# A decoder layer on one core: the embedding projection moved between the output products and the gate products, and weight blocks asked for one unit ahead

## The chip, the cores and the metric

The kernel runs on one core of one Trainium2 chip. The core has five engines that run side by side and wait for each other through semaphores: TensorE (matmuls, called PE in the profile, its weight loads PEld), VectorE (DVE), ScalarE (ACT), GpSimd (POOL) and SyncE (SP), whose queue here starts nearly all transfers between HBM and the on-chip memory. Matmuls write to eight banks of accumulators (PSUM); all else lives in the on-chip memory (SBUF). Each engine takes its instructions in the order in which the built program lists them.

The metric is the time of one execution in device microseconds, as the median of several runs. Less is better.

## What is computed

The reference is one layer of a decoder, 1024 tokens of width 1024 in float32. Cut to the parts that matter here:

```python
# h is the residual after attention: h = x + merged @ w_out
n2 = rms_norm(h, g_ffn)                                   # per token, over 1024
h = h + (silu(n2 @ w_ffn_gate) * (n2 @ w_ffn_up)) @ w_ffn_down   # D_FF = 2816
e = rms_norm(p @ w_ple_proj, g_ple)                       # p: 1024 x 256, w_ple_proj: 256 x 1024
h = h + sigmoid(h @ w_ple_gate) * e
out = rms_norm(h, g_final)
```

The embedding projection `p @ w_ple_proj` depends on inputs alone. Its result, and the per-token scale of its norm, are needed only at the very end.

## The kernel before, in words

All activations lie transposed: features over the 128 partitions, tokens along the free axis in two halves of 512 (`hf`, `hcol(hf)`). To keep float32 accuracy each operand of a matmul is split into a high part, rounded by ScalarE, and the low rest, subtracted by VectorE (`split`, lines 131 and 132), and each product is three matmuls: high by high, high by low, low by high (`passes`, lines 137 to 139). So a matmul waits for ScalarE's half of its operand, and every third one for VectorE's.

The order of the program's work: attention; the merge and the output products `po` (`w_out`, the second half of them in `out_group`); the norm's scales and the factors for the next products; gate and up products; down products; the embedding's gate and the final norm.

**Gate and up products.** They use a Strassen-Winograd scheme: for every block of 256 output features, called a unit, seven products of half size (128 x 512, four terms in the sum, so 12 matmuls of 128x512 each) take the place of eight. The right factors `Bn[1]` to `Bn[7]` (`b` in the profile) are built once from the normed `h`, in the order 1, 2, 5, 6, 7, 3, 4 that the products take them. The left factors are built for each unit from its weight block `raw` (1 MB, three buffers, tag `raw`) by sums on GpSimd (lines 918, 919, 935, 937) and then split into one of three buffers `wl`. There are 22 units, gate and up by turns, numbered `u` from 0. The first three (two gate units and an up unit, `us`) run together, product by product, since they wait for the right factors at the same time; the other 19 come from `rest()`, one after the other, with the last two products of a unit behind the first two of the next. An up unit multiplies its result with the gate's (on GpSimd, line 983), subtracts further sums on VectorE (line 976), and SP stores seven blocks per pair to `d_g` (line 973).

**Down sums.** The down products use the same scheme, so four sums of `w_ffn_down`'s blocks are formed for each of 11 values of `kk` (`down_sums`): four loads of 256 KB (line 1094), four VectorE operations (line 1097), four stores to `d_w` (line 1098). Before, a round belongs to each of the first 11 units of `rest()`, with its loads at the same place as its sums, into tiles of the ring `t` (16 buffers).

**The embedding.** `embed(hf)` loads its half of `p` and the whole of `w_ple_proj` in eight pieces, splits them, and makes eight tiles `pp` of six matmuls. ScalarE copies each (line 1072) and squares it (line 1073); the copy is stored to `d_e`, and four column sums with `ones` (line 1064, tile `pm`, on the chip eight matmuls of 128x1) add up the squares for the norm. Before, the two halves stand in the loop of `rest()`, after its units 7 and 13.

**What sets the order.** The code lists the work; a scheduler then orders the instructions of each engine at build time by a model of their times and by priority, which is the place in the code, raised in `tc.high_priority`. So an instruction can move far ahead of its place when its operands and its buffer are free. The three places shown with the change come from the built programs.

**Memory.** Eight slots of 16 KB per partition (tag `big`) go round: gate tiles, the merged activations `mT`, `wo`, then `spare` and the seven `Bn`. `spare` holds eight tiles of 512: the first four are the first snapshots of the first three units (`early_tile`), the last four `t2`, a Strassen factor; later it takes the first eight left blocks of the down products (line 1116).

## Time and profile before

| what | value |
|---|---|
| median of 3 runs | 1810.48 us (1808.75 to 1811.49) |
| the profiled execution | 1808.15 us, its span on the core 1806.4 us |
| TensorE busy | 1703.0 us, 94% of the span |
| VectorE, ScalarE, GpSimd busy | 1182.2, 906.9, 373.7 us |
| moved to and from HBM | 152.98 MB read, 67.90 MB written |
| gate and up blocks, from request to landing | 5.4 and 6.6 us in the median, 1 MB each |

How to read it: times count from the span's start. In a row of the timeline stand start, duration, engine, line, operation, written tile and read tiles, and in brackets the idle time of the engine before it and who ended it. In a table of stretches stand for each engine the busy time and the number of instructions, then the granted TensorE clock as a share of full speed and the DMA engines' share. Neighbouring matmuls overlap, so the time from start to start, not the duration, tells their rate. The last output product starts at 959.06, the first down product at 1474.25; what lies between is the part that the change touches.

### The profile page before, as it was taken

To read this page: it belongs to the slowest core of one execution; us is meant where nothing else is said; L and a number is where in the kernel's file an instruction comes from. 1 tells how busy PE (TensorE), PEld (TensorE's weight loads), DVE (VectorE), ACT (ScalarE), POOL (GpSimd) and SP (SyncE) were. 2 spreads that over 40 slices of the span, in tenths; PEclk is the share of its full clock that TensorE was granted. 3 is DMA by queue.
4 is the path that set the end of the run, shared out by engine and by line. 5 is a ranking of instruction groups with operands and counts; after the bars stand their busy time and mean duration, and the time that the engine had idled before them with its cause. 6 is when DMAs were issued, how large, how long until landed. Compare 5 with 4: busy or idle time off the path is not lost.

```text
span 1806.4 us, 23396 instructions
## 1 busy us (share of the span) xinstructions
PE 1703.0 (94%) x8148; PEld 1411.8 (78%) x8148; DVE 1182.2 (65%) x2077; ACT 906.9 (50%) x1762; POOL 373.7 (21%) x401
## 2 busy tenths in 40 slices
PE   6999999999999999996997899989899999999996
PEld 5888878888787888875886677768778878887795
DVE  6676787777876667776469766654643455556655
ACT  5275677666765767765224433333334334445421
POOL 2021210000212433332104133324323410000000
PEclk9999999999998999997998999999999999999998
DMA  5211222212314111218841265564523328664522
GB/s 169 65 58 42 55 57 59 70 53 88 111 42 153 54 60 36 65 59 315 301 159 35 83 204 193 191 211 162 192 81 132 110 93 320 192 194 164 169 70 77
DMA packets 172345, 223.21 MB, mean 124 GB/s; under 512 B 23426, under 2 KB 104322, under 8 KB 172226
## 3 DMA queue, kind: packets, MB, share of 16 engines
q1 hardware_dynamic: 166194, 201.78, 34.6%
q0 software_dynamic: 6032, 19.93, 3.0%
q8 instruction: 64, 1.05, 0.3%
q14 instruction: 55, 0.45, 0.1%
HBM read 152.98 MB, written 67.90 MB: 122 GB/s over the span
## 4 chain that ended last, share of the span: by engine, by line
PE 70%; DVE 10%; DMA 7%; issue 6%; POOL 3%; ACT 2%; SPq 1%; DVEq 0%; POOLq 0%; ACTq 0%
PE pt L137 5%; PE pt L138 5%; PE pt L139 5%; PE pd L137 4%; PE pd L138 4%; PE pd L139 4%; DMA t<-w_ffn_down 2%; PE pP L139 2%; PE pP L137 2%; PE pP L138 2%; PE tp L651 2%; DVE t L976 2%; PE po L137 1%; PE pg L139 1%; PE pg L137 1%
## 5 line engine op out<-in xcount | busy, mean ns | idle before, releaser
L137 PE MATMUL pt<-nTh,w_h 128*128 128x512 f32 (+1 forms) x480 | 191.1, 399 | 3.4 <-ACT go L355 2.3
L138 PE MATMUL pt<-nTl,w_h 128*128 128x512 f32 (+1 forms) x480 | 188.8, 393 | 0.0
L139 PE MATMUL pt<-nTh,w_l 128*128 128x512 f32 (+1 forms) x480 | 187.9, 393 | 0.0
L132 DVE TENSOR_TENSOR wl<-raw,wl 128x512 fp32r<-128x512 f32 x132 | 110.5, 837 | 117.1 <-ACT wl L131 116.7
L139 PE MATMUL pP<-b,wl 128*128 128x512 f32 x352 | 140.3, 401 | 17.2 <-DVE wl L132 17.2
L131 ACT CAST wl<-raw 128x512 fp32r<-128x512 f32 x132 | 82.1, 622 | 131.5 <-PE pP L139 63.3
L137 PE MATMUL pP<-b,wl 128*128 128x512 f32 x352 | 141.5, 402 | 4.5 <-ACT wl L131 2.6
L138 PE MATMUL pP<-b,wl 128*128 128x512 f32 x352 | 140.0, 398 | 0.0
L137 PEld LDWEIGHTS pt<-nTh,w_h 128*128 128x128 f32 (+1 forms) x480 | 90.0, 188 | 25.6 <-ACT go L355 5.6
L139 PEld LDWEIGHTS pt<-nTh,w_l 128*128 128x128 f32 (+1 forms) x480 | 89.9, 187 | 19.3
L138 PEld LDWEIGHTS pt<-nTl,w_h 128*128 128x128 f32 (+1 forms) x480 | 89.9, 187 | 18.1
L138 PE MATMUL pd<-drs,dls 128*128 128x512 f32 x296 | 102.2, 389 | 1.0 <-DVE drs L132 1.0
L139 PE MATMUL pd<-drs,dls 128*128 128x512 f32 x296 | 102.0, 389 | 0.0
L132 DVE TENSOR_TENSOR drs<-drr,drs 128x512 fp32r<-128x512 f32 x74 | 50.9, 691 | 77.3 <-ACT drs L131 77.3
L137 PE MATMUL pd<-drs,dls 128*128 128x512 f32 x296 | 99.5, 392 | 0.4 <-ACT dls L131 0.4
L131 ACT CAST drs<-drr 128x512 fp32r<-128x512 f32 x74 | 46.0, 624 | 101.5 <-PE pd L139 99.0
L139 PEld LDWEIGHTS pP<-b,wl 128*128 128x128 f32 x352 | 68.0, 193 | 35.3 <-DVE wl L132 21.0
L637 POOL TENSOR_SCALAR pw<-pw,st 128x128 f32<-128x128 f32 (+5 forms) x48 | 75.1, 1570 | 71.3 <-DVE st L633 20.1
L137 PEld LDWEIGHTS pP<-b,wl 128*128 128x128 f32 x352 | 67.8, 193 | 20.9 <-ACT wl L131 4.1
L138 PEld LDWEIGHTS pP<-b,wl 128*128 128x128 f32 x352 | 68.1, 193 | 14.1
L445 DVE TENSOR_TENSOR sz<-sz,T 128x512 f32<-128x512 f32 (+2 forms) x96 | 52.3, 550 | 35.2 <-PE T L443 34.4
L356 POOL DMA_DIRECT2D d_gate<-go x32 | 17.8, 556 | 260.9 <-ACT go L355 221.8
(371 smaller groups left out, 4831.2 us busy)
## 6 DMA issues: line engine op xcount, KB each, us to landing
d_g<-t SPq DMA_DIRECT2D x74, 256.0 KB, 2.1
drr<-d_g SPq DMA_DIRECT2D x74, 256.0 KB, 2.9
w_raw<-w_in SPq DMA_DIRECT2D x33, 512.0 KB, 4.2
raw<-w_ffn_gate SPq DMA_DIRECT2D x11, 1024.0 KB, 5.4
raw<-w_ffn_up SPq DMA_DIRECT2D x11, 1024.0 KB, 6.6
t<-w_ffn_down SPq DMA_DIRECT2D x44, 256.0 KB, 4.0
d_w<-t SPq DMA_DIRECT2D x44, 256.0 KB, 2.2
drr<-d_w SPq DMA_DIRECT2D x44, 256.0 KB, 2.7
```

The costliest lines, as they stand in the source:

```text
L131: nc.scalar.copy(out=h, in_=src)
L132: eng.tensor_tensor(out=l, in0=src, in1=r32(h), op=ALU.subtract)
L137: nc.tensor.matmul(ps, lhsT=ah, rhs=bh, start=first and i == 0, stop=False, **kw)
L138: nc.tensor.matmul(ps, lhsT=ah, rhs=bl, start=False, stop=False, **kw)
L139: nc.tensor.matmul(ps, lhsT=al, rhs=bh, start=False, stop=last and i == n - 1, **kw)
L356: nc.gpsimd.dma_start(out=dst, in_=go[0:rows, :])
L445: nc.vector.tensor_tensor(out=sz[:, c0:], in0=sz[:, c0:], in1=T[:, c0:], op=ALU.subtract)
L637: nc.gpsimd.tensor_scalar(out=pw[:, 0:nk], in0=pw[:, 0:nk], scalar1=st[:, 6:7], scalar2=None, op0=ALU.mult)
L651: nc.tensor.transpose(tp[:, i * P:(i + 1) * P], rows[i][:, kb * P:(kb + 1) * P], ident)
L976: nc.vector.tensor_tensor(out=dst, in0=a, in1=b, op=ALU.subtract)
```

## The change

It does four things.

1. The embedding's inputs are loaded and split right after the residual's loads, once: `w_ple_proj` into `wpj`, a slot of the ring `big` that stands ahead of `spare`, and both halves of `p` into two of the three `raw` buffers.
2. Both halves of the embedding are written between the output products and the gate products. Its tiles `e`, which hold copy and square side by side, share the three `wl` buffers; its `pp` tiles take four banks (`A`) and `pm` one of `B`.
3. Gate and up blocks: at the start only unit 0's is asked for; unit 1's after the first half of the embedding, which frees a `raw` buffer, unit 2's after the second. In `rest()` each block is asked for one unit ahead.
4. Down blocks go into `spare`, into its first or last four tiles by turns, asked for one unit ahead of their sums, from the third unit of `rest()` on; the down products' own loads into `spare` move behind the last round.

```diff
@@ -833,7 +833,7 @@
     def gate_up_raw(u):
         return raw_unit((w_ffn_gate, w_ffn_up)[u % 2], u // 2)
 
-    raws = {u: gate_up_raw(u) for u in range(3)}
+    raws = {0: gate_up_raw(0)}
     hs = {}
     Bn = {}
 
@@ -848,6 +848,46 @@
         for hf in range(2):
             hs[f, hf] = t_tile()
             nc.sync.dma_start(out=hs[f, hf], in_=d_h[f * P:(f + 1) * P, hcol(hf)])
+
+    wpj = slot("wpj", [P, 2, 2, D])
+    pw = []
+
+    def embed_in():
+        for k in range(2):
+            raw = wk.tile([P, 2, HALF], F32, name="praw", tag="wl", bufs=3)
+            nc.sync.dma_start(out=raw, in_=w_ple_proj[k * P:(k + 1) * P, :].rearrange("p (c n) -> p c n", n=HALF))
+            for c in range(2):
+                split(wpj[:, 0, k, hcol(c)], wpj[:, 1, k, hcol(c)], raw[:, c, :])
+        for hf in range(2):
+            pw.append(wk.tile([P, 2, 2, HALF], F32R, name="pw", tag="raw", bufs=3))
+            raw = wk.tile([P, 2, HALF], F32, name="praw", tag="wl", bufs=3)
+            nc.sync.dma_start(out=raw, in_=pT[:, hcol(hf)].rearrange("(k p) n -> p k n", p=P))
+            split(pw[hf][:, 0], pw[hf][:, 1], raw)
+
+    def embed(hf):
+        pt = ps.tile([P, HALF], F32, name="pm", **B)
+        es = []
+
+        def column_sums(f):
+            for i in range(4):
+                nc.tensor.matmul(pt[:, i:i + 1], lhsT=es[f][:, 1, i * P:(i + 1) * P], rhs=ones, start=f + i == 0,
+                                 stop=f == 7, skip_group_check=True)
+
+        for f in range(NK):
+            fs = slice(f * P, (f + 1) * P)
+            pp = ps.tile([P, HALF], F32, name="pp", **A)
+            passes(pp, [((wpj[:, 0, k, fs], wpj[:, 1, k, fs]), (pw[hf][:, 0, k, :], pw[hf][:, 1, k, :])) for k in range(2)])
+            e = wk.tile([P, 2, HALF], F32, name="e", tag="wl", bufs=3)
+            nc.scalar.copy(out=e[:, 0, :], in_=pp)
+            nc.scalar.activation(out=e[:, 1, :], in_=pp, func=AF.Square, scale=1.0 / 32.0)
+            nc.sync.dma_start(out=d_e[fs, hcol(hf)], in_=e[:, 0, :])
+            es.append(e)
+            if f:
+                column_sums(f - 1)
+        column_sums(7)
+        rstd_finish(pt, r_ple[:, 4 * hf:4 * hf + 4])
+
+    embed_in()
     spare = slot("spare", [P, 8, HALF], F32)
     t2 = [spare[:, 4 + kk, :] for kk in range(4)]
 
@@ -1002,6 +1042,10 @@
         t = next(early, None)
         return t_tile() if t is None else t
 
+    embed(0)
+    raws[1] = gate_up_raw(1)
+    embed(1)
+    raws[2] = gate_up_raw(2)
     sl = {}
     us = [gate_unit(raws[0], FIRST, early_tile, sl), up_unit(0, raws[1], FIRST, early_tile, sl)]
     sl = {}
@@ -1034,64 +1078,32 @@
 
     def rest():
         global_sl = sl
+        nxt = gate_up_raw(3)
         for u in range(3, NFF):
-            raw = gate_up_raw(u)
+            raw = nxt
+            if u + 1 < NFF:
+                nxt = gate_up_raw(u + 1)
             if u % 2:
                 yield up_unit(u // 2, raw, ORDER, t_tile, global_sl)
             else:
                 global_sl = {}
                 yield gate_unit(raw, ORDER, t_tile, global_sl)
 
-    def embed(hf):
-
-        pw = wk.tile([P, 2, 2, HALF], F32R, name="pw", tag="raw", bufs=3)
-        for k in range(2):
-            praw = t_tile()
-            nc.sync.dma_start(out=praw, in_=pT[k * P:(k + 1) * P, hcol(hf)])
-            split(pw[:, 0, k, :], pw[:, 1, k, :], praw)
-        raws = [t_tile()[:, 0:256].rearrange("p (k n) -> p k n", n=P) for _ in range(NK)]
-        for f, raw in enumerate(raws):
-            nc.sync.dma_start(out=raw, in_=w_ple_proj[:, f * P:(f + 1) * P].rearrange("(k p) n -> p k n", p=P))
-        ws = []
-        for raw in raws:
-            ws.append(wk.tile([P, 2, 2, P], F32R, name="wpj", tag="t", bufs=16))
-            split(ws[-1][:, 0], ws[-1][:, 1], raw)
-        pt = ps.tile([P, HALF], F32, name="pm", **O)
-        sqs = []
-
-        def column_sums(f):
-            for i in range(4):
-                nc.tensor.matmul(pt[:, i:i + 1], lhsT=sqs[f][:, i * P:(i + 1) * P], rhs=ones, start=f + i == 0,
-                                 stop=f == 7, skip_group_check=True)
-
-        for f in range(NK):
-            fs = slice(f * P, (f + 1) * P)
-            pp = ps.tile([P, HALF], F32, name="pp", **B)
-            passes(pp, [((ws[f][:, 0, k, :], ws[f][:, 1, k, :]), (pw[:, 0, k, :], pw[:, 1, k, :])) for k in range(2)])
-            e, sq = t_tile(), t_tile()
-            nc.scalar.copy(out=e, in_=pp)
-            nc.scalar.activation(out=sq, in_=pp, func=AF.Square, scale=1.0 / 32.0)
-            nc.sync.dma_start(out=d_e[fs, hcol(hf)], in_=e)
-            sqs.append(sq)
-            if f > 1:
-                column_sums(f - 2)
-        column_sums(6)
-        column_sums(7)
-        rstd_finish(pt, r_ple[:, 4 * hf:4 * hf + 4])
-
     KK = NFF // 2
     wd = w_ffn_down.rearrange("(k two p) n -> two p k n", two=2, p=P)
 
     def down_block(f, kh, kk):
         return wd[kh, :, kk, hcol(f)]
 
-    def down_sums(kk):
-
-        a = {}
-        for f in range(2):
-            for kh in range(2):
-                a[f, kh] = t_tile()
-                nc.sync.dma_start(out=a[f, kh], in_=down_block(f, kh, kk))
+    def down_in(kk):
+
+        a = {(f, kh): spare[:, 4 * (kk % 2) + 2 * f + kh, :] for f in range(2) for kh in range(2)}
+        for (f, kh), t in a.items():
+            nc.sync.dma_start(out=t, in_=down_block(f, kh, kk))
+        return a
+
+    def down_sums(kk, a):
+
         for i, dst, x, y, op in ((5, (1, 1), (1, 0), (1, 1), ALU.add), (7, (1, 0), (0, 0), (1, 0), ALU.subtract),
                                  (6, (0, 0), (1, 1), (0, 0), ALU.subtract), (3, (0, 1), (0, 1), (0, 0), ALU.subtract)):
             nc.vector.tensor_tensor(out=a[dst], in0=a[x], in1=a[y], op=op)
@@ -1100,8 +1112,11 @@
     LEFT = {5: 0, 6: 1, 7: 2, 3: 3}
     DIRECT = {1: (0, 0), 2: (0, 1), 4: (1, 1)}
     before = None
+    blocks = {}
     for n, u in enumerate(rest()):
 
+        if 2 <= n < KK + 2:
+            blocks[n - 2] = down_in(n - 2)
         for _ in range(2):
             next(u)
         for _ in before or ():
@@ -1109,13 +1124,11 @@
         for _ in range(3):
             next(u)
         before = u
-        if n < KK:
-            down_sums(n)
-        if n == 2:
+        if 3 <= n < KK + 3:
+            down_sums(n - 3, blocks.pop(n - 3))
+        if n == KK + 4:
             for kk in range(0, 8, 2):
                 nc.sync.dma_start(out=spare[:, kk:kk + 2, :], in_=wd[0, :, kk:kk + 2, hcol(0)])
-        if n in (7, 13):
-            embed(n // 8)
 
 
     TAGS = {"rr": ("c", 4), "rs": ("wl", 3), "ls": ("wl", 3)}
```

Where it moves instructions, as the built programs list them (`x` is the number of like rows in sequence):

TensorE at the end of the output products (`po`). Before, the first gate product (`pP`, reading the factor `b` and a left factor `wl`) follows at once:

```order
L138 MATMUL po<-mT_8838,wo 128x256
L139 MATMUL po<-mT_8838,wo 128x256
L137 MATMUL pP<-b_9222,wl 128x512
L138 MATMUL pP<-b_9222,wl 128x512
L139 MATMUL pP<-b_9222,wl 128x512
```

With the change the broadcast of a scale and then the embedding follow:

```order
L139 MATMUL po<-mT_8838,wo 128x256
L738 MATMUL bc<-acc,ones_pp 128x256
L137 MATMUL pp<-pw,wpj 128x512
L138 MATMUL pp<-pw,wpj 128x512
L139 MATMUL pp<-pw,wpj 128x512
```

All 96 matmuls of the embedding and its column sums stand here now, ahead of the first gate product.

SP around the first blocks asked for after that. With the change, from the embedding's stores on:

```order
L883 DMA d_e<-e 128x512 x4
L830 DMA raw<-w_ffn_up 128x8x256
L883 DMA d_e<-e 128x512 x9
L830 DMA raw<-w_ffn_gate 128x8x256
L883 DMA d_e<-e 128x512
L1102 DMA spare<-w_ffn_down 128x512 x4
L1110 DMA d_w<-spare 128x512 x2
L1102 DMA spare<-w_ffn_down 128x512
L1110 DMA d_w<-spare 128x512
L1102 DMA spare<-w_ffn_down 128x512
```

The blocks of units 1 and 2 stand behind the embedding's stores. The scheduler has drawn the down blocks of the rounds with odd `kk`, whose half of `spare` is free first, ahead of all stores of the units; loads and stores alternate in the queue, since a load follows the store of the tile that it overwrites. Unit 3's block stands behind 18 of these loads in all.

VectorE in the first three units, with the change (`L968` adds to a snapshot, `L1109` is a down sum, `wl` the low half of a left factor):

```order
L132 TENSOR_TENSOR b_9244<-spare,b_9244 128x256 x8
L132 TENSOR_TENSOR b_9245<-t,b_9245 128x512 x4
L132 TENSOR_TENSOR b_9246<-t,b_9246 128x512
L1109 TENSOR_TENSOR spare<-spare 128x512
L132 TENSOR_TENSOR b_9246<-t,b_9246 128x512 x2
L968 TENSOR_TENSOR spare<-pR,spare 128x512
L132 TENSOR_TENSOR b_9246<-t,b_9246 128x512
L1109 TENSOR_TENSOR spare<-spare 128x512
L132 TENSOR_TENSOR wl<-raw,wl 128x512
L132 TENSOR_TENSOR b_9247<-t,b_9247 128x512 x4
L1109 TENSOR_TENSOR spare<-spare 128x512
L132 TENSOR_TENSOR wl<-raw,wl 128x512
```

Down sums now stand among the factors and left halves of the first three units; before, the first of them stood among those of the fourth.

## The prediction

> **What bounds the kernel now.** I read the page first, then stretches of the one place that the change touches, then the chain and the waits inside them.
>
> ```profile
> PE 1703.0 (94%) x8148; PEld 1411.8 (78%) x8148; DVE 1182.2 (65%) x2077; ACT 906.9 (50%) x1762; POOL 373.7 (21%) x401
> PE 70%; DVE 10%; DMA 7%; issue 6%; POOL 3%; ACT 2%; SPq 1%; DVEq 0%; POOLq 0%; ACTq 0%
> ```
>
> TensorE sets the pace on the whole, but 94% busy does not say where it loses time. The next view does: from the last output product (959) to the end of the gate and up products (1474), cut where the kind of work changes, and a saturated stretch from the down products for scale. A second answer counts the column-sum matmuls (tile pm) in the two embedding stretches.
>
> ```profile
> core 0: us, PE busy (x) PEld busy (x) DVE busy (x) ACT busy (x) POOL busy (x), PEclk, DMA share, GB/s
> 959.00:1013.00 54.00, 38.80 (x135) 26.71 (x135) 52.81 (x98) 25.42 (x52) 21.15 (x15) 0.88 0.11 35
> 1013.00:1201.00 188.00, 179.76 (x780) 147.05 (x779) 116.09 (x145) 63.13 (x109) 67.36 (x46) 0.99 0.54 179
> 1201.00:1231.00 30.00, 22.79 (x120) 18.96 (x119) 12.05 (x19) 15.38 (x32) 4.51 (x3) 0.89 0.62 208
> 1231.00:1352.80 121.80, 115.95 (x500) 94.78 (x500) 66.34 (x84) 39.73 (x69) 45.10 (x31) 0.97 0.44 148
> 1352.80:1381.00 28.20, 25.70 (x143) 21.39 (x142) 9.81 (x15) 15.70 (x33) 7.08 (x5) 1.00 0.64 209
> 1381.00:1474.00 93.00, 92.03 (x405) 75.54 (x403) 42.43 (x61) 33.03 (x57) 34.49 (x24) 1.00 0.22 76
> 1500.00:1600.00 100.00, 100.00 (x443) 82.81 (x442) 55.78 (x89) 42.01 (x74) 0.00 (x0) 1.00 0.70 230
> ...
> 1201.00:1231.00 30.00, 6.08 (x53) 6.77 (x54) 0.00 (x0) 0.89 0.62 208
> 1231.00:1352.80 121.80, 1.43 (x13) 1.45 (x12) 0.15 (x1) 0.97 0.44 148
> 1352.80:1381.00 28.20, 7.57 (x64) 8.37 (x64) 0.00 (x0) 1.00 0.64 209
> ```
>
> The saturated row gives the price of a full matmul: 100/443 = 0.226 us. A column sum costs 6.08/53 = 0.115 us. What a stretch is longer than its matmuls at these prices is what it loses: 959 to 1013 holds some 120 full matmuls and 15 small ones, 28.6 us of work, and loses 25.4. 1013 to 1201: 780 × 0.226 = 176, loses 12. 1201 to 1231: 67 full and 53 small, 21, loses 9. 1231 to 1352.8: 487 and 13, 111.3, loses 10.5. 1352.8 to 1381: 79 and 64, 25, loses 3. 1381 to 1474: 405, 91.4, loses 1.6. Together **61.5 us lost of 515**; the rest of the program is not touched.
>
> Who takes them? In the first stretch VectorE is busy 52.8 of 54 us, and the chain of waits there (955 to 1020) is mostly its operations, the splitting of the Strassen factors (b) first:
>
> ```profile
> by line: DVE b L132 17.9%; DVE wl L132 11.6%; DVE t L845 9.8%; PE pP L139 8.7%; PE pP L137 6.4%; PE pP L138 6.3%; DVE acc L869 6.1%; issue 5.7%; DVE spare L891 4.3%; DVE t L884 4.1%; DVE acc L735 3.8%; DVE t L1020 3.7%; DVE spare L928 2.8%;
> ```
>
> In the loop a late weight block does it. Here is the longest stall, on four engines (start, duration, what ended the idle time):
>
> ```profile
> 1105.14 0.38 SPq L830 DMA_DIRECT2D raw<-w_ffn_gate  x1
> 1110.72 1.75 POOL L918 TENSOR_TENSOR s<-raw 128x512 f32<-128x512 f32 x1 [1.15 <-DMA d_w<-t]
> 1112.43 1.29 POOL L983 TENSOR_TENSOR t<-t 128x512 f32<-128x512 f32 x1
> 1113.76 2.48 DVE L976 TENSOR_TENSOR t<-t 128x512 f32<-128x512 f32 x2 [2.44 <-POOL t L983]
> 1118.09 0.50 PE L139 MATMUL pP<-b,wl 128*128 128x512 f32 x1 [3.64 <-DVE wl L132]
> ```
>
> The gate block is asked for at 1105.1. GpSimd's sum over it waits until 1110.7; the product of gate and up queues behind that sum on GpSimd, VectorE's subtraction waits for the product, and the low half of the next weights stands behind the subtraction. In the waits of 850 to 1500 the same shows in total, and the embedding's own wait beside it:
>
> ```profile
> PE pP L139 <- DVE wl L132: 17.2, 9, 3.6
> PE pp L137 <- ACT wpj L131: 8.1, 3, 6.5
> POOL s L918 <- DMA raw<-w_ffn_gate: 32.8, 7, 14.2
> SPq L973 <- POOL t L983: 134.7, 13, 19.8
> DVE t L1097 <- DMA t<-w_ffn_down: 17.7, 11, 2.9
> ```
>
> **The embedding leaves the loop.** Its inputs are now asked for and split during the output products, so its first matmul no longer waits for them:
>
> ```profile
> 1208.00 0.80 PE L137 MATMUL pp<-pw,wpj 128*128 128x512 f32 x1 [6.54 <-ACT wpj L131]
> 1209.02 0.63 PE L137 MATMUL pp<-pw,wpj 128*128 128x512 f32 x1
> 1209.44 0.63 PE L138 MATMUL pp<-pw,wpj 128*128 128x512 f32 x1
> 1211.65 0.39 PE L137 MATMUL pp<-pw,wpj 128*128 128x512 f32 x1
> 1211.88 0.39 PE L138 MATMUL pp<-pw,wpj 128*128 128x512 f32 x1
> L1072 ACT COPY t<-pp x16: 576/586/598, 1212.0 to 1375.3; 128x512 f32<-128x512 f32 x16
> L1073 ACT ACTIVATE t<-pp x16: 594/603/625, 1212.5 to 1375.8; 128x512 f32<-128x512 f32 x16
> ```
>
> After the 6.5 us gap matmuls start 0.42 us apart for 3.6 us, then 0.23: a gap costs its own length and the half clock behind it, which my 9 us hold. The work itself stays: 96 × 0.226 + 128 × 0.115 = 36.4 us of TensorE. ScalarE's two operations per tile are 0.59 + 0.60 = 1.2 us against 6 × 0.226 + 8 × 0.115 = 2.3 us of TensorE, so they hide, and with two `e` slots free (the third is held by `acc`) the store's 2.2 us fits into two tiles. Kept lost: 1.5 us; bounds 0 and 6, the last if the copies queue behind ScalarE's casts of the factors as long as that gap. The embedding pieces lost 9 + 3 = 12: **−10.5** (−12 to −6). The splits of its inputs (eight of 0.6 us on each of ScalarE and VectorE) fall under the output products, where both were a third to a half busy:
>
> ```profile
> 850.00:950.00 100.00, 100.00 (x504) 85.17 (x503) 52.21 (x86) 30.10 (x43) 10.65 (x5) 1.00 0.68 242
> ```
>
> Without that cover they would cost 5 us.
>
> **It lands where VectorE is the bound.** TensorE now has 36.4 + 28.6 = 65 us of work over the stretch in which VectorE has 52.8 and a few down sums. So VectorE should cease to be the bound, if the order lets it work ahead. By the order it does most of its factors of b5 during the embedding, then blocks on the third weight block, which is asked for only when the second half's `pw` is read out, just before the last column sums. Prices:
>
> ```profile
> raw<-w_ffn_gate SPq DMA_DIRECT2D x11, 1024.0 KB, 5.4
> t<-w_ffn_down SPq DMA_DIRECT2D x44, 256.0 KB, 4.0
> d_w<-t SPq DMA_DIRECT2D x44, 256.0 KB, 2.2
> 1004.15 5.50 DVE L132 TENSOR_TENSOR b<-t,b 128x512 fp32r<-128x512 f32 x9
> 1208.68 2.10 DVE L132 TENSOR_TENSOR wpj<-t,wpj 128x256 fp32r<-128x256 f32 x6 [0.27 <-ACT wpj L131]
> ```
>
> A split is 5.50/9 = 0.61 us on VectorE, a half one 0.35. Let E be the end of the embedding's column sums. The block is asked for some 2.5 us before E and lands at E + 2.9; its low half is ready at E + 4.2, and TensorE wants it after two units' first products, 24 × 0.226 = E + 5.4: no stall. Then VectorE has, in its order, one weight split, eight half splits of b6 (2.8), four of b7 (2.4), four of b3 (2.4), two down sums and an addition before the second unit's second low half: E + 14.7. TensorE wants that at 4 products × 2.7 + eight matmuls = E + 12.7: stall 2.0. Behind it b4 (2.4) and a down sum precede the third unit's: about 1 more. Ahead of these, ScalarE's high halves cost up to 1. I take **5 us** lost in place of 25.4, **−20.4**. Bounds: 2 (only the first stall) and 18 (VectorE finds only its work on b5, some 30% of the stretch, ready during the embedding, and the other 70% of the old loss returns after it).
>
> **Down sums are the added wait.** Eleven rounds of four sums are no longer held to the units from the fourth on; five of them stand in VectorE's queue among the first three units' weight splits, which wait behind them, and TensorE behind those. A round's cycle is known from here:
>
> ```profile
> 1197.84 1.86 SPq L1094 DMA_DIRECT2D t<-w_ffn_down  x4
> 1204.22 1.42 DVE L1097 TENSOR_TENSOR t<-t 128x512 f32<-128x512 f32 x2 [2.04 <-DMA t<-w_ffn_down]
> ```
>
> From the first request to the first sum 6.4 us, four sums 2.6, a store 2.2: 11 us in series, and piece by piece (a block's request follows its own store) some 8 to 9. The five rounds meet 17 products, 46 us, 9.2 a round. So VectorE waits one or two us in a round, and the three weight buffers (5.4 us of products) cover it. I put nothing on the path here beyond the 5; if the cover is gone, five rounds × 2 = 10, which the 18 above holds. The Trainium skill's page "PSUM — Partial Sum Buffer", section "Engine vs sequencer instructions", says that ScalarE, VectorE and GpSimd queues are strictly first in, first out: by it a late down block holds every weight split behind it. The four waits above agree, and the rule speaks against this change.
>
> **The loop's late blocks.** Gate and up blocks are asked for one unit (7 × 12 × 0.226 = 19 us) earlier, against 5.4 us to land and a block that came 3.6 us late in the stall above. The request needs a buffer freed two units back, and in SP's queue stores of the products stand ahead of it, which waited for GpSimd up to 19.8 us: a whole unit, though that wait is itself the late block's. I take it that the request goes out in time. What remains I read from 1381 to 1474, the loop without down sums: 1.6/93 = 1.7%, so 5 us on 310 in place of 22.5: **−17.5** (−20.5 if only 2 remain; −8.5 if SP's stores eat the unit's lead for two blocks in three and 14 remain).
>
> **Sum.** −10.5 − 20.4 − 17.5 = −48.4. The profiled execution took 1808.15 us (span 1806.4), so 1759.8; the median shown, 1810.48, lies 2.3 above it, so **1762 us**. Ends: −12 − 23.4 − 20.5 = −56, 1754; −6 − 7.4 − 8.5 = −22, 1788.
>
> **Rivals.**
>
> 1. *VectorE stays the bound at the turn.* For it: 52.8 of 54 us busy, and ScalarE now copies 32 embedding tiles (19 us) between its casts. Against it: 36 us more of TensorE work lie there. The gain at the turn falls to the 7.4 of the bound: 1775.
> 2. *The loop's stalls stay.* If the down sums on VectorE and not the late blocks held the weights, only the two moves gain: 1810.5 − 10.5 − 20.4 = 1780. The waits for down blocks, 17.7 us, speak for it, and that 1381 to 1474, without them, loses so little; the row at 1110.72 and GpSimd's 32.8 us speak against it.
> 3. *Slower: the down rounds run in series.* One half of `spare` holds a whole round, and SP's queue interleaves its requests with stores that wait for VectorE. If each block's request, landing, sum and store follow one another (4.0 + 0.6 + 2.2 = 6.8 us), the 20 blocks of the early rounds take 136 us where 46 are at hand, TensorE loses 90, and the time is 1762 + 90 = 1852. It decides from 94 us for the 20 blocks, 4.7 a block: then the whole gain is gone. Against it: in the last rows four blocks overlap, 6.4 us to the first sum. The queue rule named above is what would make this stall whole.
>
> **Chances.** My forecast 0.73, rival 1 0.11, rival 2 0.09, rival 3 0.04, an effect that I did not see and that returns about the time of before 0.03. Range 1750 to 1787: below the best sum by the scatter of the runs (2.7 us), above it to the bad end and both milder rivals. About 0.2% (3.6 us) is what a measurement of this kernel can tell from no change: faster 0.93, same 0.03, slower 0.04.
>
> **What would show it.** Right: no gap of several us before the first `pp`; VectorE's share in the 40 us after the last output product well under 1; GpSimd's waits for gate and up blocks near zero; the gate loop's stretch without column sums at 1.7% lost. Wrong at the turn: gaps of TensorE behind `wl` in the first three units of more than 5 us together, or VectorE idle before line 1109 for more than 15. Rival 2: the same 3 us gaps every two units. Rival 3: weight blocks of the fourth unit landing after its first product is due, 57 us after E.

## The result, and the profile after

The change takes 1783.78 us (median of 4 runs, 1782.32 to 1785.67) where the kernel before takes 1810.81 (1808.75 to 1811.49, 4 runs): a ratio of 0.9853, 95% interval 0.9836 to 0.9870. It is faster, by 27.0 us; 48.4 were forecast. The forecast of 1762 lies 22 us below.

First the stretch between the last output product and the first down product, which begins at 961.3 and ends at 1451.8: 490.4 us where it was 515.2. In a row stand the limits, the length, the busy time and number of instructions of each engine, the granted TensorE clock, the DMA share and GB/s.

```profile
961.00:1001.00 40.00, 39.73 (x243) 34.53 (x242) 29.45 (x73) 23.04 (x48) 20.89 (x7) 1.00 0.44 150
1001.00:1031.00 30.00, 23.13 (x85) 18.12 (x84) 25.35 (x37) 17.23 (x35) 18.00 (x10) 0.83 0.41 140
1031.00:1170.00 139.00, 126.83 (x532) 102.50 (x531) 86.05 (x115) 44.79 (x79) 45.74 (x32) 0.96 0.72 243
1170.00:1381.00 211.00, 208.54 (x916) 171.03 (x915) 99.61 (x135) 74.64 (x130) 83.67 (x60) 1.00 0.32 106
1381.00:1452.00 71.00, 69.81 (x307) 57.20 (x306) 33.27 (x48) 25.66 (x44) 23.28 (x17) 1.00 0.21 75
```

At 0.226 us for a full matmul and 0.115 for a column sum the embedding (961 to 1001, 115 and 128 of them) loses next to nothing, the turn (1001 to 1031) 30 - 85 × 0.226 = 10.8 us, the loop up to 1170 18.8, up to 1381 4.0, and the rest 1.6. Added up from start to start of all matmuls the stretch loses 38.0 us; before it lost 62.3 in the same measure, and the prediction kept 1.5 + 5 + 5 = 11.5. That measure is called "lost" below, and goes with each profile.

Next the waits of TensorE in that stretch, and those of VectorE up to 1170 (engine, tile and line that waited, what it waited for; total us, times, longest):

```profile
PE pP L139 <- DVE wl L132: 10.1, 9, 4.0
PE pR L139 <- DVE wl L132: 5.8, 1, 5.8
PE pP L137 <- DVE t L968: 3.2, 2, 2.5
```

```profile
DVE spare L1109 <- DMA spare<-w_ffn_down: 25.8, 13, 6.1
```

TensorE still waits for the low halves of weights. Nothing of several us stands ahead of the first embedding product, and VectorE is busy 29.45 of the 40 us behind the last output product instead of nearly all: those two signs of the prediction came true. The 5.8 us at the turn and VectorE's 25.8 us at the down sums were its signs of having gone wrong there. GpSimd's waits for gate blocks, over the whole stretch, fell as forecast, from 32.8 us:

```profile
POOL s L958 <- DMA raw<-w_ffn_gate: 8.1, 8, 1.4
```

The waits for up blocks fell from 89.2 to 42.8 us, 28.0 of them in one wait, and not to near zero, as that sign would have it. And the loop loses 24.4 us (18.8 + 4.0 + 1.6), as much as the 24.1 (12 + 10.5 + 1.6) that the prediction read before. That is 5.8% of its 421 us where 1.7% was named: the first hint that the late blocks had not been its stalls.

### The profile page after: what moved, and what is told of

Its sections match the earlier page's. It is cut to its first block, busy times and chain, and to the rows that moved or that the text cites. A ratio compares the mean times of both kernels' runs of the same rounds, so it can differ in the third digit from the quotient of the medians.

```text
span 1784.0 us, 23325 instructions
## 1 busy us (share of the span) xinstructions
PE 1697.2 (95%) x8148; PEld 1410.5 (79%) x8148; DVE 1157.2 (65%) x2063; ACT 901.7 (51%) x1748; POOL 389.7 (22%) x401
## 4 chain that ended last, share of the span: by engine, by line
PE 74%; DVE 9%; issue 6%; DMA 5%; POOL 2%; ACT 2%; SPq 1%; POOLq 0%; DVEq 0%; ACTq 0%
PE pt L137 5%; PE pt L138 5%; PE pt L139 5%; PE pd L138 4%; PE pd L137 4%; PE pd L139 4%; PE pP L139 3%; PE pP L137 3%; PE pP L138 3%; DMA spare<-w_ffn_down 2%; PE po L137 2%; PE tp L651 2%; PE po L138 2%; PE po L139 2%; PE pg L139 2%
## 5 line engine op out<-in xcount | busy, mean ns | idle before, releaser
L132 DVE TENSOR_TENSOR wl<-raw,wl 128x512 fp32r<-128x512 f32 x132 | 95.4, 723 | 101.9 <-ACT wl L131 101.4
L637 POOL TENSOR_SCALAR pw<-pw,st 128x128 f32<-128x128 f32 (+5 forms) x48 | 75.0, 1569 | 71.6 <-DVE st L633 20.2
```

The lines of the kernel that those rows point to most:

```text
L132: eng.tensor_tensor(out=l, in0=src, in1=r32(h), op=ALU.subtract)
L637: nc.gpsimd.tensor_scalar(out=pw[:, 0:nk], in0=pw[:, 0:nk], scalar1=st[:, 6:7], scalar2=None, op0=ALU.mult)
```

## The experiments

All times are medians, ratios are to the kernel before in the same round of runs, with 95% intervals. "Stretch" and "lost" are of the profiled execution, as above. In three of these executions (the change without down sums, the change with GpSimd's sums held, the embedding alone with differences later) some 5 us of "stretch" and "lost" come of a slower clock in the embedding, told at the end. Lists of stalls count them from start to start of the matmuls, which makes each up to 0.2 us longer than the idle time in its row of the timeline (4.2 for 4.00).

| kernel | time, us | ratio | stretch, us | lost, us |
|---|---|---|---|---|
| before | 1810.8 | | 515.2 | 62.3 |
| the change | 1783.8 | 0.9853 (0.9836 to 0.9870) | 490.4 | 38.0 |
| embedding alone | 1787.0 | 0.9884 (0.9860 to 0.9908) | 491.9 | 39.5 |
| gate and up ahead alone | 1797.8 | 0.9934 (0.9919 to 0.9949) | 504.4 | 51.5 |
| both, down rounds as before | 1787.2 | 0.9879 (0.9850 to 0.9909) | 491.2 | 38.8 |
| the change without down sums | 1773.1 | 0.9800 (0.9773 to 0.9827) | 479.9 | 27.5 |
| the change, rounds held | 1794.0 | 0.9920 (0.9898 to 0.9942) | 498.2 | 45.8 |
| the change, GpSimd's sums held | 1787.5 | 0.9882 (0.9859 to 0.9906) | 498.4 | 46.0 |
| embedding alone, GpSimd's sums held | 1777.2 | 0.9824 (0.9805 to 0.9843) | 481.9 | 29.5 |
| that, differences later | 1759.3 | 0.9721 (0.9697 to 0.9745) | 464.4 | 11.9 |
| that, down sums taken apart too | 1757.9 | 0.9708 (0.9681 to 0.9735) | 464.3 | 11.9 |
| embedding alone, differences later | 1760.4 | 0.9728 (0.9703 to 0.9753) | 469.3 | 16.9 |
| before, differences later | 1789.8 | 0.9884 (0.9859 to 0.9910) | 496.4 | 43.6 |
| the change, differences later | 1775.2 | 0.9803 (0.9776 to 0.9830) | 479.1 | 26.7 |

### Which part gave the gain

The first theory was that the rounds drawn forward hold VectorE and so take back what the rest gains. Two kernels take parts of the change away. In both a round's loads stand with its sums again and go into the ring t; against the change:

```diff
-        if 2 <= n < KK + 2:
-            blocks[n - 2] = down_in(n - 2)
...
-        if 3 <= n < KK + 3:
-            down_sums(n - 3, blocks.pop(n - 3))
+        if n < KK:
+            down_sums(n)
```

> The embedding stands between output and gate products and gate and up blocks are asked for one unit ahead, as in the change; the down rounds are as before (loads beside their sums, in the ring t, one round for each of the units 3 to 13). Theory (the down rounds that were drawn forward hold VectorE, and the weights' low halves behind it): the five gaps of 1.9 to 5.9 us between 1010 and 1155 shrink to under 1 us each, the loop from 1031 on loses about 8 us in place of 25, the time is 1766 to 1772. Rival (the weight blocks are late behind SP's stores, whatever the rounds do): gaps stay, 1780 to 1787. Rival (the gain is all the embedding's): the loop loses 20 or more as before, 1783 or more.

The second also asks for gate and up blocks in their own unit again:

```diff
-            raw = nxt
-            if u + 1 < NFF:
-                nxt = gate_up_raw(u + 1)
+            raw = gate_up_raw(u)
```

> The embedding is moved, with unit 1's and 2's blocks behind its halves; nothing in the loop is asked for ahead and the down rounds are as before. Theory: the embedding's move is worth what the turn and the two pieces gained in the change, some 15 + 11 us, and the loop's stalls of 22 us stay: 1783 to 1787. If late weight blocks never held the loop: as the first kernel of this call, 1766 to 1772.

They measured 1787.2 and 1787.0 us, stretches 491.2 and 491.9; the second is what was expected of the embedding's move, the first is not. The embedding's move alone brings 23.8 of the change's 27.0 us; asking for gate and up blocks a unit ahead adds nothing to it, and putting the rounds back gains nothing, it costs 3 us, less than the intervals tell. The theory fell. Both kernels show a stall of 2.0 to 4.0 us every two units, as rival 2 of the prediction had it:

```profile
PE pP L139 <- DVE wl L132: 17.1, 8, 3.9
```

```profile
PE pP L139 <- DVE wl L132: 19.4, 8, 3.9
```

(TensorE's waits in the stretch, first with both parts and then with the embedding alone; before, the five that lie in the loop were 12.2 us.)

The third takes VectorE's 44 down sums out of the change:

```diff
-            nc.vector.tensor_tensor(out=a[dst], in0=a[x], in1=a[y], op=op)
             nc.sync.dma_start(out=d_w[LEFT[i], kk], in_=a[dst])
```

> The change with VectorE's 44 down sums left out: blocks are loaded and stored as they are, so the down products work on other numbers. Theory (VectorE stands before a sum whose block has not landed): the gaps of the first three units and of 1049 to 1151 fall below 1 us, 1762 to 1768. Rival (SP's queue holds the weight blocks): SP still alternates loads and stores, gaps stay, 1778 to 1784. 44 operations of 0.6 us off VectorE alone, with no wait, would give nothing, since it is busy 65%.

1773.1 us, 10.7 less than the change and between the theory and its rival: VectorE's queue matters in the loop. Behind a stall that ends 112 us into the stretch none is left, where the change has two more of 4.2 and 2.8.

The fourth holds a round's loads on SP behind the next gate or up request, and its sums on VectorE behind the latest weight split, so that neither can be drawn forward (`asked` holds the last such request, `halved` the last low half):

```diff
-            blocks[n - 2] = down_in(n - 2)
+            with tc.issue_after(asked[0]):
+                blocks[n - 2] = down_in(n - 2)
...
-            down_sums(n - 3, blocks.pop(n - 3))
+            with tc.issue_after(halved[0]):
+                down_sums(n - 3, blocks.pop(n - 3))
```

> The change with each round held to its unit: its loads stand on SP behind the request for the next unit's weight block, its sums on VectorE behind the latest low half of a left factor; buffers and lead of one unit as in the change. Theory: the loads land a unit before their sums, VectorE does not wait for them, the first three units are free of sums; 1760 to 1768, faster than the change by 16 to 24 us. Rival (late weight blocks, or the alternation of loads and stores in one half of spare): 1778 to 1787.

1794.0 us, slower than the change: a miss. VectorE no longer stands at a late down block, but the stalls every two units are back, seven of 1.0 to 5.2 us, and longer than with the embedding alone. So something else than down blocks makes those stalls, and it grows with this edit. VectorE's waits from 1040 to 1400 name a candidate, GpSimd's product of gate and up, for which the differences behind it wait:

```profile
DVE t L1020 <- POOL t L1027: 18.0, 9, 4.2
```

(Lines 1020 and 1027 are 1016 and 1023 of the change.)

### Is it the late gate and up blocks?

The kernel before with the request a unit ahead and nothing else, the same edit as above read backwards:

> The kernel before with one edit: inside the loop a unit's gate or up block is asked for at the start of the unit ahead of it. The embedding stays in the loop, the down blocks are asked for as before. Theory of the prediction (the place in the program sets when a block is asked for): the loop's four late blocks go, 1810.8 - 17.5 = about 1793, stretch from the last output product to the first down product about 498 instead of 515.2. Rival, the ring of three buffers: every request waits for the split that frees its buffer (in the kernel before it is then 31 to 38 us ahead of the first use of the block's sum), and the four late ones (8.0, 16.9, 8.0 and 19.1 us ahead) are late because the embedding's two word tiles stand in that ring; asked a unit sooner, the request waits for the same split. Then the time stays at 1811 within 4 us, and four blocks are still asked for less than 20 us ahead.

1797.8 us, between the two theories, and both were wrong about it. Before, an up block is asked for 8.0 us ahead of the split of its sum, and that split waits for GpSimd; with the edit the same block is asked for 30.6 us ahead. First before, then the edit (SP's request, ScalarE's split):

```profile
1208.67 0.42 SPq L830 DMA_DIRECT2D raw<-w_ffn_up  x1
1216.71 0.62 ACT L131 CAST wl<-s 128x512 fp32r<-128x512 f32 x1 [0.26 <-POOL s L918]
```

```profile
1169.10 0.38 SPq L830 DMA_DIRECT2D raw<-w_ffn_up  x1
1199.70 0.62 ACT L131 CAST wl<-s 128x512 fp32r<-128x512 f32 x1
```

So the place in the program does set when the four blocks beside the embedding are asked for. But the stalls are not theirs. TensorE's waits from 1040 to 1400, first before, then with the edit:

```profile
PE pP L139 <- DVE wl L132: 12.2, 5, 3.6
PE pp L137 <- ACT wpj L131: 8.1, 3, 6.5
```

```profile
PE pP L139 <- DVE wl L132: 15.1, 7, 3.4
PE pp L137 <- ACT t L1076: 0.3, 1, 0.3
```

The waits for low halves stay. What goes is the embedding's wait for its own inputs, 8.1 us, which the move of the embedding takes away too: hence nothing is left for this edit once the embedding has gone. (Why the request's place brings the embedding's splits forward was not followed.) In the loop of the change the request can't go out earlier at all. SP's waits for the split that frees a `raw` buffer, 1075 to 1450, before and after:

```profile
SPq L830 <- DVE wl L132: 20.6, 11, 6.6
```

```profile
SPq L830 <- DVE wl L132: 83.0, 15, 6.6
```

With three buffers a block of the loop, from unit 5 on, is asked for 32 to 37 us ahead of the split of its sum in the change, and 32 to 36 with the embedding alone. A fourth buffer wasn't tried.

### The order of GpSimd, then of VectorE

With the embedding alone one stall reads like this, on VectorE, GpSimd, ScalarE and TensorE:

```profile
1178.63 2.49 DVE L1016 TENSOR_TENSOR t<-t 128x512 f32<-128x512 f32 x2 [1.18 <-POOL t L1023]
1181.04 0.68 DVE L968 TENSOR_TENSOR t<-pR,t 128x512 f32<-128x512 f32 x1
1181.64 0.68 DVE L1016 TENSOR_TENSOR t<-t 128x512 f32<-128x512 f32 x1
1182.24 0.69 DVE L132 TENSOR_TENSOR wl<-raw,wl 128x512 fp32r<-128x512 f32 x1
```

```profile
1175.62 1.29 POOL L958 TENSOR_TENSOR s<-raw 128x512 f32<-128x512 f32 x1 [0.88 <-DMA raw<-w_ffn_gate]
1176.86 1.74 POOL L1023 TENSOR_TENSOR t<-t 128x512 f32<-128x512 f32 x1
1178.56 1.29 POOL L959 TENSOR_TENSOR raw<-raw 128x512 f32<-128x512 f32 x1
...
1176.67 0.62 ACT L131 CAST wl<-raw 128x512 fp32r<-128x512 f32 x1 [2.10 <-PE pR L139]
```

```profile
1182.98 0.50 PE L139 MATMUL pP<-b,wl 128*128 128x512 f32 x1 [3.17 <-DVE wl L132]
```

ScalarE has the weights' high half at 1177.3; the low half comes at 1182.9. In between VectorE waits 1.2 us for GpSimd's product and works through three differences and an addition; the differences are needed by nothing but the stores to `d_g`. (The first two took 2.49 us and not 1.41, since GpSimd's next sum was under way; the last section has it.) The product is late since GpSimd first stood 0.9 us at a block that has just been asked for and then summed it, a sum that is not needed for 25 us. Two links can be cut: GpSimd's order or VectorE's.

First GpSimd's, in the change and in the embedding's move alone:

```diff
+        with tc.issue_after(prods[-3]) if len(prods) > 2 else ExitStack():
             G.tensor_tensor(out=s1, in0=a21, in1=a22, op=ALU.add)
             G.tensor_tensor(out=a21, in0=a11, in1=a21, op=ALU.subtract)
...
-                nc.gpsimd.tensor_tensor(out=g, in0=g, in1=u, op=ALU.mult)
+                d = nc.gpsimd.tensor_tensor(out=g, in0=g, in1=u, op=ALU.mult)
+                prods.append(d.ins)
```

> The changed kernel with one edit: on GpSimd a unit's two block sums (lines 958 and 959) may not stand ahead of the gate times up product of the up unit before last; nothing else is held, and all work is done. Theory (GpSimd's queue): what is left of the loop's stalls comes from GpSimd standing at the sum over a block that has just been asked for, 25 us before anyone needs that sum, while a product that VectorE's difference waits for stands behind it. Then the stalls of 4.2, 2.8 and 1.0 us at 165, 190 and 310 us after the last output product fall below 1 us each: stretch 490.4 to about 482, time 1784 to about 1776. Rival (VectorE's load): the down sums fill VectorE, GpSimd's order is no matter: stretch 488 to 492, time within 3 us of 1784.

> The embedding's move alone, nothing asked for ahead, with the same edit on GpSimd: a unit's two block sums stand behind the product of the up unit before last. Without the edit this kernel has six stalls of 2.0 to 4.0 us, one every two units, stretch 491.9, time 1787. Theory (GpSimd's queue): the six fall below 1 us each, stretch to about 476, time to about 1771, under the kernel with the rounds drawn forward. Rival (VectorE's load by the down rounds): six stalls of 2 us and more stay, time within 4 us of 1787.

In the change it gains nothing (1787.5 us; stalls of 5.3 and 2.8 us stay where 4.2 and 2.8 were). With the embedding alone it brings 9.8 us, but the six stalls shrink from 19.5 to 12.6 us together and don't vanish: 1.7 to 2.8 each, where under 1 was expected. Half right.

Then VectorE's. A difference is now written not at its product but five weight splits later, and held behind that split's low half (`lows` lists the low halves so far, `LATE` is 5, and `later(low)` issues what is due, behind `low`):

```diff
         def sub(i, dst, a, b):
-            nc.vector.tensor_tensor(out=dst, in0=a, in1=b, op=ALU.subtract)
-            done[i] = dst
-            store(i, dst)
+            def go():
+                nc.vector.tensor_tensor(out=dst, in0=a, in1=b, op=ALU.subtract)
+                store(i, dst)
+            done[i] = dst
+            due.append((len(lows) + LATE, go))
...
+            low = split(w[:, 0], w[:, 1], left[i])
+            lows.append(low.ins)
+            later(low.ins)
```

> The embedding's move alone with GpSimd's sums held back, and one more edit: VectorE's differences of an up unit's products (line 1016 of the changed kernel), which only the stores to d_g need, stand five weight splits later in its queue. The kernel without this edit has six stalls of 1.7 to 2.8 us, 12.6 us together, stretch 481.9, time 1777. Theory (VectorE's order: a difference that waits for GpSimd's product stands ahead of the low half of a split that TensorE waits for): the six fall under 1 us each, stretch to about 473, time to about 1768. Rival (VectorE's load over two units, whatever the order): the six move behind another product and keep their length, time within 3 us of 1777.

1759.3 us, nine less than the theory had it, stretch 464.4, and no stall in the loop. From 1030 to 1381, and the waits of TensorE in the whole stretch:

```profile
1030.00:1175.00 145.00, 145.00 (x641) 120.11 (x640) 85.49 (x113) 53.68 (x93) 59.35 (x40) 1.00 0.57 187
1175.00:1381.00 206.00, 206.00 (x910) 170.65 (x909) 122.65 (x160) 75.80 (x130) 85.52 (x58) 1.00 0.49 165
```

```profile
PE pR L139 <- DVE wl L132: 3.9, 1, 3.9
PE pR L137 <- ACT wl L131: 1.1, 1, 1.1
PE pp L137 <- DVE t L903: 0.3, 1, 0.3
```

641 × 0.226 = 144.9 of 145 us and 910 × 0.226 = 205.7 of 206: TensorE is the bound there and nothing else, with VectorE busy 59% and 60% of the time. So the rival, VectorE's load whatever the order, is out: its operations are the same, only their order is not. (Less work cures it too: the change without down sums has no stall behind 112 us, and there the differences stand where they stood.) All three waits left lie ahead of the loop. The same place, one pair of units, in VectorE's queue (lines 1029 and 978 are 1016 and 968 of the change; 132 the low halves):

```profile
1167.33 1.18 DVE L132 TENSOR_TENSOR wl<-raw,wl 128x512 fp32r<-128x512 f32 x1
1168.86 0.69 DVE L978 TENSOR_TENSOR t<-pR,t 128x512 f32<-128x512 f32 x1 [0.36 <-PE pR L139]
1169.52 0.69 DVE L132 TENSOR_TENSOR wl<-raw,wl 128x512 fp32r<-128x512 f32 x1
1172.72 0.69 DVE L132 TENSOR_TENSOR wl<-s,wl 128x512 fp32r<-128x512 f32 x1 [2.51 <-ACT wl L131]
1173.33 1.41 DVE L1029 TENSOR_TENSOR t<-t 128x512 f32<-128x512 f32 x2
```

The differences now come behind the low halves, and TensorE waits for none of them. There they also meet GpSimd's operations at other times; how much of the gain is the wait for the product and how much the 1.1 us for which GpSimd's sum held two differences was not told apart.

Taking the four down sums of a round apart on top, each behind another split (the second to the fifth after the round's loads), brings no more that shows:

> The same kernel with the differences five splits later, and the four down sums of a round also taken apart: each stands behind another weight split, the second to the fifth after the round's loads are asked for, where they stood in pairs. Theory (VectorE's order): what the differences alone left is gone, stretch 470 to 473, time 1765 to 1768. Rival (VectorE's load): as without it, 1777 within 3 us.

1757.9 us. The interval overlaps the one without it, and the stretch is the same to 0.1 us: no difference that these runs can tell. It is the lowest time measured, 26 us under the change.

### Which kernel needs which order

Three last kernels have the differences later and nothing held on GpSimd: in the embedding's move alone, in the kernel before, and in the change.

> The embedding's move alone with the differences five splits later; GpSimd's sums stand where they stood. Theory (VectorE's differences are the cause, GpSimd's order only made them later): the six stalls of 2.0 to 4.0 us fall under 1 us, stretch 464 to 467, time 1759 to 1763. Rival (GpSimd's order is a cause of its own): half of the stalls' 19.5 us stays, stretch about 475, time about 1770.

> The kernel before with the differences five splits later; embedding, gate, up and down blocks as before. Theory (the five stalls every two units before, 1.8 to 3.8 us, 13.0 us together, came of the differences and not of late gate and up blocks): they fall under 1 us, the turn (24 us) and the embedding's pieces stay, stretch about 500, time about 1796. Rival (the prediction's step: late gate and up blocks): the five stay, time within 4 us of 1811.

> The change as it stands, with VectorE's differences of an up unit's products put five weight splits later in its queue and nothing else altered. In the change the two largest stalls of the loop (4.2 and 2.8 us) end where VectorE stands at a down sum whose block has not landed (3.0 and 3.5 us), with weight splits behind it, and no difference is near. Theory (two orders of VectorE's queue: differences in the kernels with the rounds as before, late down blocks in the change): those stalls stay, about 6 us of smaller losses go, stretch about 484, time about 1778. Rival (the differences alone): as in the kernels with the rounds as before, stretch about 466, time 1760.

With the embedding alone: 1760.4 us, and TensorE waits nowhere from 1030 to 1400. GpSimd's order is not needed: it only decided how late the differences were. (The stretch, 469.3, is 5 us longer than the one above by a slower clock in the embedding, told at the end.)

In the kernel before: 1789.8 us, about 20 less, and the stalls every two units are gone with no block asked for earlier. From 1040 to 1400 TensorE's waits for low halves are

```profile
PE pP L139 <- DVE wl L132: 0.4, 1, 0.4
```

where they were 12.2. The turn (some 24 us) and the embedding's pieces stay.

In the change: 1775.2 us. (In this kernel one difference of unit 3 reads a tile of `spare` into which a down block has been loaded meanwhile, so its values are others; the operations and their number are the same.) Of the two stalls that the theory kept one stays, 3.8 us, and the turn is no better. What holds VectorE there is its down sums, up to 1170:

```profile
DVE spare L1123 <- DMA spare<-w_ffn_down: 35.2, 16, 6.3
```

(Line 1123 is 1109 of the change.) The same in the change itself, around its stall of 4.0 us, on VectorE, SP and TensorE:

```profile
1123.77 1.00 DVE L132 TENSOR_TENSOR wl<-raw,wl 128x512 fp32r<-128x512 f32 x1 [1.10 <-ACT wl L131]
1128.30 0.69 DVE L1109 TENSOR_TENSOR spare<-spare 128x512 f32<-128x512 f32 x1 [3.52 <-DMA spare<-w_ffn_down]
1128.91 0.68 DVE L968 TENSOR_TENSOR t<-pR,t 128x512 f32<-128x512 f32 x1
1129.51 0.68 DVE L132 TENSOR_TENSOR wl<-raw,wl 128x512 fp32r<-128x512 f32 x1
...
1123.58 2.62 SPq L1102 DMA_DIRECT2D spare<-w_ffn_down  x4
...
1130.24 0.50 PE L139 MATMUL pP<-b,wl 128*128 128x512 f32 x1 [4.00 <-DVE wl L132]
```

Four loads go out at 1123.6, the first sum over them waits until 1128.3, and the addition and the low half stand behind it. The loads come late because their tiles are still being stored; SP's waits up to 1170 have it:

```profile
SPq L1102 <- DMA d_w<-spare: 25.1, 19, 4.6
```

So the change and the other kernels lose time in the loop by two different orders of VectorE's queue, and drawing the rounds forward exchanged the one for the other: putting the differences later takes 1787.0 - 1760.4 = 26.6 us from the embedding's move alone, but only 1783.8 - 1775.2 = 8.6 from the change, where down blocks hold the queue at the turn and in the first units of the loop. Without the differences in the way the rounds drawn forward, and the earlier requests with them, cost 1775.2 - 1760.4 = 14.8 us; with the differences in place they gained 1787.0 - 1783.8 = 3.2, which the intervals don't tell from nothing.

## Why the prediction was right or wrong

**What bounds the kernel.** The reading of the stall was right link by link: block asked for, GpSimd's sum, product, difference, low half, TensorE. The choice of the link to blame was wrong. The prediction took the first, the late block, since the chain begins there. The block's sum was not needed for 25 us; what made its lateness felt was that work which only feeds stores, the difference, stood ahead of the low half. The chain names all who waited, and not which of them had to.

**The embedding leaves the loop** (-10.5 forecast, 1.5 us kept). Right: no wait for its inputs is left, and 1.2 us are lost up to the end of the column sums. That ScalarE's two copies and the splits hide was right too.

**It lands where VectorE is the bound** (-20.4, 5 us kept). The mechanism was right, the size off: the turn keeps 10.8 us, so it gave 14.6. The term mis-sized is VectorE's work ahead of the second unit's second low half, forecast to end 14.7 us behind E, the end of the column sums. E was 1000.1, and the low half ended at 1020.26, 20.2 behind. The half splits of b6 (eight in one row), that low half and the matmul that waited:

```profile
1007.40 4.97 DVE L132 TENSOR_TENSOR b<-spare,b 128x256 fp32r<-128x256 f32 x8
1019.58 0.68 DVE L132 TENSOR_TENSOR wl<-raw,wl 128x512 fp32r<-128x512 f32 x1
1020.31 0.80 PE L139 MATMUL pR<-b,wl 128*128 128x512 f32 x1 [5.76 <-DVE wl L132]
```

Three parts of the 5.5 us can be read. The eight half splits, taken at 0.35 us each, took 0.62 in the mean: six as priced, and two 1.5 us each, while GpSimd worked on weights from 1007.6 to 1010.4. They began 7.3 us behind E where the prediction's times give 4.8: the two weight splits ahead of them, priced at 0.61 us, took 1.17 and 1.30 beside GpSimd's sums, and the first of them began 0.9 us late, since ScalarE's half before it waited for a store of the embedding to release the weight buffer. And 0.6 us went in waiting for a down block. What GpSimd's work does to VectorE is told in the last section. The other losses of the turn are 1.1 us for a high half and some 3.2 of half clock, 1.4 of them with no gap ahead. Down sums make 1.9 us of the stall: where they aren't drawn forward, the 5.8 us are 3.9. The third block was in time, as priced (asked for at 997.6, landed 5.6 us later, ahead of the stall).

The two moves together can be read without the differences in the way: before against the embedding alone, both with differences later, 1789.8 to 1760.4 = -29.4 us; forecast were 10.5 + 20.4 = 30.9. So the first two steps were nearly right, and in the change as made part of it is covered by the stalls that stay.

**Down sums: nothing on the path.** Failed. The prediction gave each round a cycle of 8 to 9 us and let three weight buffers cover one or two us of waiting; VectorE waited 25.8 us at 13 places, up to 6.1 at one, more than the 5.4 us of products in the buffers. The order of VectorE's queue decided: in the rows above 4.00 us of TensorE stand behind 3.52 of VectorE. The Trainium skill's page "PSUM — Partial Sum Buffer", section "Engine vs sequencer instructions", has that queue strictly first in, first out; the trace agrees. Rival 3 was this at its worst, and its price of 90 us was far too high, for four blocks do overlap.

**The loop's late blocks** (-17.5, "I take it that the request goes out in time"). Failed twice. The request doesn't go out earlier: the ring of three sets it, 83.0 us of SP's waits. And it would not have helped: with the four late blocks in time the stalls were still 15.1 us. That the loop's stalls could be won back, and about as much of them, was right by luck, for another cause: the differences alone are worth about 20 us on the kernel before and 26.6 on the embedding's move. The 1.7% that the prediction took as unavoidable in the loop went with them; 0.3 of 206 us is what remains.

**Rivals.** The nearest was rival 2, the loop's stalls stay, 1780 us, with a chance of 0.09. It blamed the down sums; that is half of it in the change, and not the cause before. The two facts weighed against it, the chain at 1110.72 and GpSimd's 32.8 us, were read as late blocks. That 1783.8 us lies within the stated 1750 to 1787 is no merit of the third step, which brought nothing: the first two carry the gain, and the upper end had been drawn to take in the milder rivals. Sum: 11.5 us kept by the prediction against 38.0 measured, 5.8 more at the turn and 19 in the loop, and the rest by the finer count.

## What to carry to other kernels

When a chain of waits runs over several in-order queues, ask of each link whether the work in it is needed by the next: an operation that feeds only a store, ahead of one that the bound engine waits for, is the link to cut, and moving it behind cost nothing here. Asking for data earlier helps only where the buffer is free earlier; look at what the request itself waits for. A gain and a new loss of the same size can cancel, so try each part of a change alone, and once more with the next stall out of the way.

## What the runs showed of the hardware

**VectorE and GpSimd hold each other up.** Two differences took 2.49 us while GpSimd worked, from 1178.56 to 1179.85, and 1.41 in the kernel with them later, where GpSimd was idle; both rows stand above. The pair ended at 1178.63 + 2.49 = 1181.12, 1.27 us behind GpSimd's end, about a pair's own length: as if it had begun when GpSimd was done. The same holds throughout the embedding alone from 1030 to 1400: all 51 VectorE operations of 128x512 with both inputs in SBUF that began with more than 0.2 us of a GpSimd operation to go ended 0.55 to 0.56 us behind its end, however much was left of it, while the 11 with one input in PSUM took 0.69 us, as they do with GpSimd idle. It goes the other way too: one GpSimd operation of the change (line 977), 1.41 us long at 1007.56, took 5.90 from 1020.34, where VectorE worked without a pause. The Trainium skill's page "SBUF — State Buffer", section "Who interferes with whom", says that a VectorE instruction with two inputs in SBUF contends with a GpSimd instruction that reads SBUF, and that the ports they share are an exclusive lock; the trace agrees. It had not been in the prediction's price of the half splits.

**The clock can fall with TensorE never idle.** In the profiled execution of the embedding alone with differences later, the second half of the embedding:

```profile
963.00:990.00 27.00, 26.73 (x154) 22.71 (x153) 18.60 (x49) 14.82 (x32) 10.60 (x5) 1.00 0.45 161
990.00:1006.00 16.00, 16.00 (x79) 14.15 (x78) 9.43 (x22) 7.57 (x16) 9.39 (x2) 0.68 0.28 92
```

TensorE is busy 16.00 of 16 us and is granted 0.68 of its clock; matmuls start 0.43 us apart instead of 0.23. It cost some 5 us there and in the two others named under the table, and about 1.5 in most of the rest that have the embedding there: in the change seven matmuls start 0.43 us apart from 1001.3 on, with no gap ahead. Stretches of single executions are to be compared with this in mind. The prediction allowed half clock only behind a gap. That the many small column sums between the products bring it about is a guess that no run here tested; what speaks for it is that 24 of them stand in a row just ahead in the change, from 997.4 to 1000.1.
